# Two modulation vectors as one-column products: weights as the left operand, summed over all input tiles in PSUM

## The chip, the cores and the metric

The kernel runs on one core of a Trainium2 chip. The metric is the device time of one execution in microseconds (us). Besides DMA, five engines work side by side, each through its own queue of instructions: PE (matrix products into PSUM; PEld is its loading of the left operand), DVE and ACT (elementwise work, both read PSUM), POOL (elementwise work in SBUF) and SP, which here issues the weight transfers. They wait for one another through semaphores.

## The reference, cut to what matters

The program is a two-layer encoder over 256 positions of width 2048: an RWKV-7 layer, then a band-attention layer, each with an MLP. A vector `c` modulates every sub-layer.

```python
D_MODEL = 2048; SEQ = 256; DEPTH = 2
def modulate(h, shift, scale):
    return h * (1 + scale[:, None, :]) + shift[:, None, :]

for layer in range(DEPTH):
    mod = c @ w_ada[layer] + b_ada[layer]            # (1, 6 * 2048)
    sh1, sc1, gt1, sh2, sc2, gt2 = jnp.split(mod, 6, axis=-1)
    ...
    h = modulate(rms_norm(x, g_mix[layer]), sh1, sc1)
    y = rwkv7_time_mix(h, ...)      # layer 0: v = (h + xx * mu[3]) @ w_v, and so on
    x = x + gt1[:, None, :] * y
    h = modulate(rms_norm(x, g_mlp[layer]), sh2, sc2)
    x = x + gt2[:, None, :] * sq_relu_mlp(h, w_up[layer], w_down[layer])
return rms_norm(x, g_final)
```

The change concerns `sh1` and `sc1` of layer 0 alone: 2 x 2048 numbers, each a sum over 2048 inputs, from 32 MB of f32 weights.

## The kernel before, in words

Everything is laid out with features on the 128 partitions: a vector of 2048 is a [128, 16] tile whose column n is "tile n", and activations are [128, 16, 256]. Large products are made of fp32r halves: a weight tile is split by `halves` into wH (ACT, L362) and wL (DVE, L365), an activation by `split` into two halves (ACT L536, DVE L537), and three partial products are summed in PSUM.

The first stage is `layer_a` (L593), about the first 220 us. It computes `sh1` and `sc1` (parts 0 and 1) in eight blocks of two tiles, in the generator `ada_blocks` (L623). For each block and part, four transfers of 512 KB (L635, tile `rawa`, four buffers) bring [128 inputs, 4 input tiles, 256 outputs] each, so a block has eight transfers and the stage 64. For each of the four input tiles one f32 product (L639) has 32 copies of `c`'s column (tile `crep`, made once by DVE at L617) as its left operand and 256 columns of weights as the moving one. Input tile kt uses column tile kt mod 4 of the array (`tile_position=(0, g)`), so four products stand side by side, and the sums lie in PSUM as rows: 32 equal rows for each of four groups of input tiles. After 16 input tiles ACT copies the rows to SBUF (L645), and 16 products of one column with the constant 1/32 (L650, `col(C_32ND)`) turn them into columns and add up the four groups. DVE adds the bias (L656, twice) and makes the gain (L658).

The PSUM tile of these sums, tag `m`, has one buffer; the norm's `rstd` (L489) uses it too. The norm of the first tile needs the first block, and tile n of the norm needs block n/2: DVE scales (L718), ACT shifts (L720), POOL makes the difference to the position before (L675), DVE mixes (L680), then PE runs the LoRA products (L727, L731, f32) and the value products: `v` (L735 to L737, by rows, 24 a tile) and `t` (`v_part`, L699 to L701, 24 a tile from tile 4 on), whose sums ACT copies (L705) or DVE adds (L707).

The order on each engine is made by a scheduler from the order of issue; the generator is advanced in the loop over tiles (L709), one transfer's products at a time, ahead of the tile that needs the block. Later modulation vectors are made in another way: DVE accumulates the weighted rows (L425), and `ada_sum` (L432) turns them into columns with 32 one-column products (L437), whose left operand is 32 columns of the accumulated tile. The rest (RWKV pairs, output product, MLP, attention) is not touched by the diff.

## Time and profile before

| what | value |
|---|---|
| median of 3 runs | 2769.86 us (2765.64 to 2773.61) |
| the profiled execution | 2776.48 us, of which the span from first to last instruction is 2774.7 |
| PE busy | 2666.3 us, 96% |
| DVE, ACT, POOL busy | 2120.3 us (76%), 1277.1 (46%), 286.7 (10%) |
| HBM traffic | 237 GB/s over the span |
| mean granted TensorE clock | 0.986 |

The views: the page sums an execution up. "Groups" put the instructions of one line and shape together: count, busy time, mean ns of one, then the idle time of the engine before them and what ended it (`<-`). "Windows" give each engine's busy time, with the number of its records, in a stretch of time. "In order of time" lists one engine's instructions with start and length, like ones merged (`x8`). A product's left operand of "128x32" has 128 rows and 32 columns; an f32 product leaves more than one MATMUL record. "issue" as a releaser means that the engine waited for nothing that the profile shows.

### The profile page before, as it was taken

To read this page: it belongs to the slowest core of one execution; us is meant where nothing else is said; L and a number is where in the kernel's file an instruction comes from. 1 tells how busy PE (TensorE), PEld (TensorE's weight loads), DVE (VectorE), ACT (ScalarE), POOL (GpSimd) and SP (SyncE) were. 2 spreads that over 40 slices of the span, in tenths; PEclk is the share of its full clock that TensorE was granted. 3 is DMA by queue.
4 is the path that set the end of the run, shared out by engine and by line. 5 is a ranking of instruction groups with operands and counts; after the bars stand their busy time and mean duration, and the time that the engine had idled before them with its cause. 6 is when DMAs were issued, how large, how long until landed. Compare 5 with 4: busy or idle time off the path is not lost.

```text
span 2774.7 us, 58075 instructions
## 1 busy us (share of the span) xinstructions
PE 2666.3 (96%) x23594; PEld 2236.9 (81%) x23594; DVE 2120.3 (76%) x3161; ACT 1277.1 (46%) x2253; POOL 286.7 (10%) x416
## 2 busy tenths in 40 slices
PE   6999999999999999999999999998999999999997
PEld 3677777777888888888888888776888888888886
DVE  4568678788899888788888997799997566565665
ACT  2345455555445434344344454465454344443454
POOL 0003343353210000000000100000100000000002
PEclk9999999999999999999999999999999999999999
DMA  9876456554686889898898878888867555555553
GB/s 300 279 268 193 153 184 190 169 182 150 211 303 226 304 304 304 292 308 306 299 313 288 294 245 278 277 264 271 282 229 269 184 189 188 185 189 185 187 188 123
DMA packets 217389, 662.62 MB, mean 239 GB/s; under 512 B 21409, under 2 KB 68897, under 8 KB 217121
## 3 DMA queue, kind: packets, MB, share of 16 engines
q1 hardware_dynamic: 215056, 656.36, 71.3%
q8 instruction: 185, 3.03, 0.4%
q10 hardware_dynamic: 2064, 2.54, 0.3%
q14 instruction: 84, 0.68, 0.1%
HBM read 656.72 MB, written 2.10 MB: 237 GB/s over the span
## 4 chain that ended last, share of the span: by engine, by line
PE 79%; DVE 7%; DMA 6%; issue 4%; ACT 2%; POOL 1%; DVEq 0%; ACTq 0%; POOLq 0%
PE pj L396 41%; PE pj L397 21%; DMA raw<-w_ada 3%; DVE wL L365 3%; DMA raw<-w_ada_kv 2%; PE iv L105 2%; PE gr L99 1%; DVE acc L425 1%; PE m L639 1%; PE o L385 1%; PE ms L99 1%; ACT wH L362 1%; POOL sL L117 1%; PE o L387 1%; PE py L320 1%
## 5 line engine op out<-in xcount | busy, mean ns | idle before, releaser
L396 PE MATMUL pj<-aHL,wH 128*128 128x512 f32 x3520 | 1282.1, 404 | 8.7 <-ACT wH L362 6.5
L362 ACT CAST wH<-raw 128x1024 fp32r<-128x1024 f32 x772 | 807.2, 1046 | 973.2 <-PE pj L396 611.2
L365 DVE TENSOR_TENSOR wL<-raw,wH 128x1024 fp32r<-128x1024 f32 x772 | 943.6, 1225 | 270.7 <-ACT wH L362 267.8
L397 PE MATMUL pj<-aHL,wL 128*128 128x256 f32 x3520 | 993.2, 282 | 2.4 <-DVE wL L365 2.3
L396 PEld LDWEIGHTS pj<-aHL,wH 128*128 128x128 f32 x3520 | 666.5, 189 | 170.3 <-issue 10.1
L396 PE MATMUL pj<-hHL,wH 128*128 128x512 f32 x2048 | 725.4, 399 | 4.3 <-DVE hHL L906 4.3
L397 PEld LDWEIGHTS pj<-aHL,wL 128*128 128x128 f32 x3520 | 666.7, 189 | 5.6 <-DVE wL L365 4.0
L397 PE MATMUL pj<-hHL,wL 128*128 128x256 f32 x2048 | 574.6, 281 | 4.8 <-DVE wL L365 4.7
L425 DVE SCALAR_TENSOR_TENSOR acc<-raw,ct,acc 128x1024 f32<-128x1024 f32 x360 | 467.0, 1297 | 123.5 <-DMA raw<-w_ada 83.3
L396 PEld LDWEIGHTS pj<-hHL,wH 128*128 128x128 f32 x2048 | 385.3, 188 | 100.4 <-DVE hHL L906 6.7
L397 PEld LDWEIGHTS pj<-hHL,wL 128*128 128x128 f32 x2048 | 387.4, 189 | 7.1 <-DVE wL L365 6.7
L484 POOL TENSOR_TENSOR ss<-ss,sq 128x256 f32<-128x256 f32 x56 | 52.0, 929 | 1615.5 <-ACT sq L483 1615.2
L931 DVE SCALAR_TENSOR_TENSOR x<-pj,mod,x 128x256 f32<-128x256 f32 x256 | 123.2, 481 | 51.6 <-PE pj L397 48.6
L905 ACT CAST hHL<-t 128x256 fp32r<-128x256 f32 x128 | 51.6, 403 | 61.2 <-DVE t L904 60.2
L639 PE MATMUL m<-rawa,crep 128*32 128x256 f32 x512 | 47.2, 448 | 16.8 <-DMA rawa<-w_ada 16.3
L387 PE MATMUL pj<-aHL,wL 128*128 128x258 f32 x192 | 55.9, 293 | 6.9 <-DVE wL L365 6.9
L385 PE MATMUL pj<-aHL,wH 128*128 128x258 f32 x192 | 56.2, 293 | 2.2 <-ACT wH L362 1.6
L386 PE MATMUL pj<-aHL,wH 128*128 128x258 f32 x192 | 56.3, 293 | 0.0
L906 DVE TENSOR_TENSOR hHL<-t,hHL 128x256 fp32r<-128x256 f32 x128 | 53.4, 417 | 1.4 <-ACT hHL L905 1.4
L904 DVE SCALAR_TENSOR_TENSOR t<-t 128x256 f32<-128x256 f32 x120 | 50.7, 422 | 2.7
L881 DVE TENSOR_TENSOR t<-pj,t 128x256 f32<-128x256 f32 x120 | 50.0, 417 | 0.5 <-ACT t L880 0.5
L241 POOL TENSOR_TENSOR al<-da,csts 128x128 f32<-128x128 f32 x64 | 41.1, 652 | 68.8 <-PE iv L105 64.1
(246 smaller groups left out, 2792.6 us busy)
## 6 DMA issues: line engine op xcount, KB each, us to landing
raw<-w_ada SPq DMA_DIRECT2D x320, 512.0 KB, 4.9
raw<-w_up SPq DMA_DIRECT2D x256, 512.0 KB, 4.8
raw<-w_down SPq DMA_DIRECT2D x256, 512.0 KB, 4.3
rawa<-w_ada SPq DMA_DIRECT2D x64, 512.0 KB, 6.6
raw<-w_ada_kv SPq DMA_DIRECT2D x64, 512.0 KB, 5.6
raw<-w_k SPq DMA_DIRECT2D x32, 512.0 KB, 4.4
raw<-w_r SPq DMA_DIRECT2D x32, 512.0 KB, 4.6
raw<-w_o SPq DMA_DIRECT2D x32, 512.0 KB, 5.0
```

Source lines behind the costliest of these rows:

```text
L99: self.b.nc.tensor.matmul(o(c)[K], lhsT(c)[K], rhs(c)[K], start=True, stop=True)
L105: self.b.nc.tensor.matmul(o[QS[K], c, :], lhsT[QS[R], c, :], rhs[QS[R], c, :], start=True, stop=True, tile_position=(H * R, H * K))
L362: nc.scalar.copy(Hf, raw)
L365: eng.tensor_tensor(out=Lf, in0=raw, in1=Hf, op=ALU.subtract)
L385: nc.tensor.matmul(ps, H[:, i, :], a(kt)[:, 0, :], start=(first and kt == 0), stop=False)
L386: nc.tensor.matmul(ps, H[:, i, :], a(kt)[:, 1, :], start=False, stop=False)
L387: ins = nc.tensor.matmul(ps, L[:, i, :], a(kt)[:, 0, :], start=False, stop=(last and kt == KT - 1))
L396: nc.tensor.matmul(ps, H[:, i, :], a(kt), start=(kt == 0), stop=False)
L397: ins = nc.tensor.matmul(ps[:, 0, :], L[:, i, :], a(kt)[:, 0, :], start=False, stop=(kt == KT - 1))
L425: nc.vector.scalar_tensor_tensor(out=acc, in0=raw, scalar=ck, in1=acc, op0=ALU.mult, op1=ALU.add)
L639: nc.tensor.matmul(ps[g:g + 32, part, :W], crep[:, kt, :], raw[:, i, :], start=(part == 1 and kt < 4), stop=(part == 0 and kt >= KT - 4), ...
L931: nc.vector.scalar_tensor_tensor(out=x, in0=ps[:, i, :], scalar=self.mods[(layer, 5)][:, n:n + 1], in1=x, op0=ALU.mult, op1=ALU.add)
```

## The change

Weights and `c` swap places. A product now has 32 columns of the weights as its left operand and one column of `c` as the moving one, so that its sum is already a column of 32 outputs. The four column tiles of the array are the four groups of 32 outputs of a tile. All 16 input tiles add up in the same PSUM column; column `part * w_ + n` of the tile `m` holds part `part` of the block's n-th tile. A transfer has 4 input tiles x 2 tiles x 4 groups = 32 such products in place of 4, so 2048 in place of 256 over the stage. `crep`, the copy `adat`, the 128 products with 1/32 and that constant are gone, and the bias is added from the first PSUM tile.

```diff
-    put("cols", np.tile(np.array([RMS_EPS, GN_EPS, -0.5, 1.0, 1 / 32], np.float32), (P, 1)))
+    put("cols", np.tile(np.array([RMS_EPS, GN_EPS, -0.5, 1.0], np.float32), (P, 1)))
...
-            crep = pb.tile([P, KT, 32], F32, name="crep")
-            nc.vector.tensor_copy(crep, self.ct.unsqueeze(2).to_broadcast([P, KT, 32]))
...
-                    ps = self.psm().rearrange("p (i n) -> p i n", i=2)
+                    ps = self.psm()
...
                                 kt = ks * a + i
-                                g = 32 * (kt % 4)
-                                nc.tensor.matmul(ps[g:g + 32, part, :W], crep[:, kt, :], raw[:, i, :],
-                                                 start=(part == 1 and kt < 4), stop=(part == 0 and kt >= KT - 4),
-                                                 tile_position=(0, g))
+                                for n in range(w_):
+                                    for g in range(0, P, 32):
+                                        nc.tensor.matmul(ps[g:g + 32, part * w_ + n:part * w_ + n + 1],
+                                                         raw[:, i, n * P + g:n * P + g + 32], self.ct[:, kt:kt + 1],
+                                                         start=(part == 1 and kt == 0 and n == 0),
+                                                         stop=(part == 0 and kt == KT - 1 and n == w_ - 1),
+                                                         tile_position=(0, g))
...
-                    t = pb.tile([P, 2 * T], F32, tag="adat", bufs=1, name="adat").rearrange("p (i n) -> p i n", i=2)
-                    nc.scalar.copy(t[:, :, :W], ps[:, :, :W])
-                    ps = self.psm()
-                    for part in range(2):
-                        for i in range(w_):
-                            for g in range(0, P, 32):
-                                nc.tensor.matmul(ps[g:g + 32, 2 * part + i:2 * part + i + 1],
-                                                 t[:, part, i * P + g:i * P + g + 32], self.col(C_32ND),
-                                                 start=True, stop=True, tile_position=(0, g))
...
-                        nc.vector.tensor_tensor(out=self.mods[(0, part)][:, o], in0=ps[:, 2 * part:2 * part + w_],
+                        nc.vector.tensor_tensor(out=self.mods[(0, part)][:, o], in0=ps[:, part * w_:(part + 1) * w_],
```

In the changed file the new products are at L638, the adds of the bias at L648.

More of the change, by code (lines that the diff above doesn't have):

```diff
@@ L72 @@
 QS = [slice(H * i, H * i + H) for i in range(4)]
-C_RMS, C_GN, C_MHALF, C_ONE, C_32ND = range(5)
+C_RMS, C_GN, C_MHALF, C_ONE = range(4)
 class Pair:
```

## The prediction

> **What bounds the kernel now.** I read the page first (busy shares, the DMA queues), then the groups of the first 220 us, where all the changed lines run, then that stage by windows and PE's instructions in order of time.

> ```profile
> span 2774.7 us, 58075 instructions
> ...
> PE 2666.3 (96%) x23594; PEld 2236.9 (81%) x23594; DVE 2120.3 (76%) x3161; ACT 1277.1 (46%) x2253; POOL 286.7 (10%) x416
> ...
> q8 instruction: 185, 3.03, 0.4%
> ```
> ```profile
> L639 PE MATMUL m<-rawa,crep 128*32 128x256 f32 x512 | 47.2, 448 | 16.8 <-DMA rawa<-w_ada 16.3 <-DVE rv L491 0.5
> L650 PE MATMUL m<-csts,adat 128*32 128x1 f32 x256 | 3.6, 175 | 0.9 <-ACT adat L645 0.9
> ```
> ```profile
> core 0: us, PE busy (x) PEld busy (x) DVE busy (x) ACT busy (x) POOL busy (x), PEclk, DMA share, GB/s
> 97.00:118.00 21.00, 20.13 (x188) 14.65 (x191) 10.54 (x20) 6.28 (x11) 1.34 (x2) 1.00 0.82 286
> 142.00:165.00 23.00, 21.41 (x206) 15.86 (x207) 13.97 (x30) 7.23 (x12) 1.88 (x2) 1.00 0.92 310
> ```

> PE is busy 96% of the span, and within the first stage 20.13 of 21 us and 21.41 of 23. So there too PE sets the pace: what a changed product costs in PE's order is paid, and DVE and ACT, half idle, matter only where PE waits for them. The first 25 us are paced by DMA instead (below). The groups show 512 records for 256 products of L639 and 256 records for 128 of L650: an f32 product makes two MATMUL records, and as many LDWEIGHTS.

> **The change part by part.** Per 512 KB transfer of weights, four products that move 256 columns (L639) become 32 that move one (L638 of the changed file), with tile shape and operands like L437, which this kernel already runs in batches of 32. Per block of two tiles, one ACT copy (L645) and 16 products (L650) go. There are 64 transfers and eight blocks; SP's and POOL's queues keep their order, so no DMA moves past another.

> *PE time of a batch*, from PE's instructions in order of time: the old batch, the new batch's likeness, and the removed one.

> ```profile
> 151.34 0.28 PE L737 MATMUL v<-aHL,wL 128*128 128x256 f32 x1
> 151.55 0.64 PE L639 MATMUL m<-rawa,crep 128*32 128x256 f32 x8
> 152.12 0.39 PE L735 MATMUL v<-aHL,wH 128*128 128x256 f32 x1
> 152.34 0.28 PE L736 MATMUL v<-aHL,wH 128*128 128x256 f32 x1
> 152.46 0.28 PE L737 MATMUL v<-aHL,wL 128*128 128x256 f32 x1
> ```
> ```profile
> 913.14 0.28 PE L397 MATMUL pj<-aHL,wL 128*128 128x256 f32 x1
> 913.34 0.71 PE L437 MATMUL m<-csts,acc 128*32 128x1 f32 x64
> 913.99 0.50 PE L396 MATMUL pj<-aHL,wH 128*128 128x512 f32 x1
> 914.32 0.28 PE L397 MATMUL pj<-aHL,wL 128*128 128x256 f32 x1
> 914.44 0.40 PE L396 MATMUL pj<-aHL,wH 128*128 128x512 f32 x1
> 914.68 0.28 PE L397 MATMUL pj<-aHL,wL 128*128 128x256 f32 x1
> ```
> ```profile
> 164.00 0.28 PE L699 MATMUL t<-aHL,wH 128*128 128x256 f32 x1
> 164.22 0.43 PE L650 MATMUL m<-csts,adat 128*32 128x1 f32 x32
> 164.80 0.28 PE L701 MATMUL t<-aHL,wL 128*128 128x256 f32 x1
> ```

> Undisturbed starts are 0.12 us apart (152.34, 152.46). With four L639 products between, 151.34 to 152.34 is 1.00 where two starts make 0.24: the batch costs 0.76 us. With 32 L437 products, 913.14 to 914.32 is 1.18 where a wide and a narrow pitch (914.32 to 914.68) make 0.36: 0.82, so +0.06 a transfer. The L650 batch costs 0.80 - 0.24 = 0.56. In seven blocks that run against a dense PE: 56 x 0.06 - 7 x 0.56 = 3.4 - 3.9 = **-0.5 us**. On PE time the change is a tie.

> Accumulating one column over 16 tiles has no row here (L437 starts and stops each product). Its bounds: 0 (L437's two records already add into one address), and at most the old 0.76 doubled, since four column tiles overlap either way. I take 0.

> [...] 64 MATMUL records took 0.65 us, 10 ns each. [...]

> *The shorter chain at a block's end.* The modulation waits for the block's last product.

> ```profile
> 92.90 0.64 PE L639 MATMUL m<-rawa,crep 128*32 128x256 f32 x8
> 94.38 0.43 PE L650 MATMUL m<-csts,adat 128*32 128x1 f32 x32
> 97.23 0.39 PE L699 MATMUL t<-aHL,wH 128*128 128x256 f32 x1 [0.79 <-ACT v L705]
> 99.08 0.67 PE L727 MATMUL l<-mix,lw 128*96 128x256 f32 x2 [0.63 <-DVE mix L680]
> ```

> From the end of L650 (94.81) to the first L727 of the next tile are 4.3 us, through DVE, ACT and POOL; PE waits 0.79 + 0.63 = 1.42 of them. The change starts this 4.3 at the last product instead, 1.3 us earlier (93.47 to 94.81). But in the new order the 26 products of v that stood on both sides of L650 all follow the last product: 3.1 us of cover against 4.3, a wait of 1.2 instead of 1.42. That is -0.2 x 7 = **-1.5 us**. Bounds: 0, and the full 1.3 x 7 = -9.

> *The start.*

> ```profile
> 20.88 1.08 PE L639 MATMUL m<-rawa,crep 128*32 128x256 f32 x8 [0.42 <-DMA rawa<-w_ada]
> 22.38 1.08 PE L639 MATMUL m<-rawa,crep 128*32 128x256 f32 x8 [0.42 <-DMA rawa<-w_ada]
> 25.00 0.58 ACT L645 COPY adat<-m 128x512 f32<-128x512 f32 x1 [6.54 <-PE m L639]
> 25.64 0.60 PE L650 MATMUL m<-csts,adat 128*32 128x1 f32 x32 [0.70 <-ACT adat L645]
> ```

> The first block's transfers come 1.5 us apart and nothing covers its end: copy and L650 (25.00 to 26.24) go, -1.2. The copy of crep (L617) is off the path, since L639 waited for its weights.

> *What the change adds that no busy time shows: PE's instructions themselves.* The page has 23594 + 23594 PE and PEld records, and queue q8 brought 185 packets, 3.03 MB: 255 records, 16 KB a packet. So q8 is PE's instruction stream, in blocks of 256. It can be late:

> ```profile
> 264.39 0.34 PE L105 MATMUL iv<-u,xs 32*32 32x32 f32 x17
> 264.99 0.38 PE L105 MATMUL iv<-u,xs 32*32 32x32 f32 x15 [0.27 <-issue]
> ```
> ```profile
> 738.12 0.38 PE L105 MATMUL iv<-u,xs 32*32 32x32 f32 x20
> 738.88 0.31 PE L105 MATMUL iv<-u,xs 32*32 32x32 f32 x12 [0.38 <-issue]
> ```
> ```profile
> 264.98:362.98 98.00, 93.32 (x1651) 71.50 (x1651) 70.68 (x129) 45.83 (x126) 40.01 (x49) 0.91 0.53 166
> 362.98:738.87 375.89, 369.80 (x7115) 288.89 (x7115) 304.52 (x566) 198.32 (x557) 149.31 (x200) 0.99 0.57 178
> 262.76:266.14 3.38, 2.65 (x70) 2.10 (x71) 3.38 (x8) 0.98 (x3) 2.25 (x2) 0.85 0.54 162
> 733.05:736.43 3.38, 3.38 (x101) 2.79 (x90) 2.35 (x4) 1.69 (x4) 0.00 (x0) 1.00 0.88 316
> ```

> Batches of 32 independent products break off in the middle, with "issue" as the only releaser, at 264.99, 363.00 and 738.88. Between the breaks lie 3302 and 14230 records, 26 and 106 short of 13 and 56 blocks of 256; PE's semaphore instructions fill that up. So each break stands at a block's border. The DMA view, narrowed to 0.01 or 0.02 us, finds one q8 packet at 262.76 (its row:

> ```profile
> q8 instruction: 1, 0.02, 603.8%
> ```

> Before, the stage fetched 12 blocks in 186 us, which hid every round:

> ```profile
> q8 instruction: 12, 0.20, 0.5%
> ```

> The new products make 4 records each: (2048 - 256 - 128) x 4 = 6656 more, 26 more blocks. Inside a run of new batches, one batch and the 8.5 products of v after it are 128 + 17 records in 0.82 + 8.5 x 0.12 = 1.8 us, so 256 in 3.2 us: less than a round. A block's eight batches stand in two runs (five and three) and hold (8 x 128 + 6 x 17)/256 = 4.4 instruction blocks; the first of each run was fetched during the stretch before it, leaving 2.4. The stage's DMA share, 0.82 to 0.92, is like the slow round, but a stopped PE releases no buffers and thins the DMA, so I take the middle round, 4.6: 2.4 x (4.6 - 3.2) x 7 = **+24 us**. At 3.4 it is 2.4 x 0.2 x 7 = +3, at 5.7 +42. At the start eight batches are four blocks, at two transfers (3.0 us) each; two of them must be fetched: 2 x 1.6 = +3.2, with the -1.2 above **+2**.

> [...]

> Sum: -0.5 - 1.5 + 24 + 2 = +24 on the profiled execution's 2776.5 us. That stands 6.6 above the median; on the median of 2769.9 it gives 2794.

> **The rivals.** *Fetches stay hidden* (more than one block ahead, the three breaks chance): -0.5 - 1.5 - 1.2 = -3, **2767**. For it: no break in the stage before. Against: two breaks exactly whole blocks from the first. Chance 0.16.
> *Faster:* fetches hidden, and each block's end gains its whole 1.3 us, because PE waits for the chain and nothing else: -9 - 1.2 - 0.5 = -11, **2759**. It decides from 1 us a block's end on. Against: the new order puts the same 26 products there, and one of the two waits was for ACT's L705, not the chain. Chance 0.05.
> *The granted clock falls*, since a one-column batch keeps the array emptier. For it: a cold L639 batch (1.08 us at 20.88, 0.64 at 151.55) shows that PE does slow after sparse work. Against: the L437 and L650 batches left the next pitch at 0.12. If a quarter of the seven blocks' 96 products x 0.12 = 11.5 us doubled: +20 without any late fetch, **2790**. Chance 0.08.
> [...]

> **How the numbers follow.** Late fetches get 0.69, of which 0.03 lie at rounds near 3.4 us, below +8. A change under 0.3% (8.3 us) can't be told from none. Slower: 0.66 + 0.08 + 0.02 = 0.76; same 0.16 + 0.03 = 0.19; faster 0.05. The range runs from the hidden fetch (2767) past the slow round (-0.5 - 1.5 + 42 with a start of +4: 2814) to 2820. For late fetches alone it would be 2772 to 2814.

> **What would show it.** Right: q8 with 211 packets, PE with 26922 records; batches of L638 broken off inside by "issue" without any releaser; PEld's idle time by "issue" up by tens of us; blocks of 25 to 27 us instead of 23 (94.38 to 164.22, three blocks); all later stages as long as before. Wrong: L638 batches unbroken at 0.65 us each and blocks of 23 us (hidden); pitches of 0.24 in v's products between batches (clock); batches evenly stretched to 1.6 us (floor).

## The result and the profile after

The changed kernel takes 2816.84 us (median; 2814.87 to 2820.34) against 2769.56 us before: a ratio of 1.017, 95% interval 1.0152 to 1.0187, so 47 us slower. The profiled execution took 2820.34 us.

From the page of the changed kernel, the lines that answer to the first fence of the prediction:

```profile
span 2818.6 us, 64722 instructions
...
PE 2691.7 (96%) x26922; PEld 2289.7 (81%) x26922; DVE 2120.5 (75%) x3160; ACT 1272.3 (45%) x2245; POOL 293.7 (10%) x416
...
q8 instruction: 211, 3.46, 0.5%
```

PE's records rise by 3328, PEld's by as many, and q8 brings 26 packets more: the forecast's 26922 and 211 exactly. PE's share stands at 96% in both kernels. A share of busy time does not show this loss.

Windows show where it lies. First the kernel before, its first stage from 26 us on and everything behind it; then the changed kernel (columns as in the prediction; the last three are granted clock, DMA share and GB/s):

```profile
26.00:220.00 194.00, 177.20 (x1591) 131.24 (x1584) 112.46 (x219) 68.62 (x107) 14.41 (x16) 0.98 0.81 271
220.00:2774.00 2554.00, 2480.10 (x21928) 2103.65 (x21926) 2000.94 (x2926) 1199.90 (x2129) 272.07 (x396) 0.99 0.71 236
```
```profile
30.00:261.00 231.00, 201.37 (x4487) 178.50 (x4482) 112.70 (x218) 64.94 (x99) 13.73 (x16) 0.85 0.69 225
261.00:2818.00 2557.00, 2481.93 (x21928) 2103.41 (x21928) 2001.39 (x2927) 1199.67 (x2130) 279.73 (x396) 0.99 0.71 235
```

Behind the first stage both run the same 21928 PE records in 2554 and 2557 us. The first stage, without its start, went from 194 to 231 us, its start from 26 to 30: 41 of the profiled span's 44 us. Two things are new in that row: PE is idle for 30 us instead of 17, and the granted clock (that column of the windows, a share of full speed) is 0.85 instead of 0.98. The pace of the blocks stands in the starts of the bias adds (first and last start of 16 instructions, two a block), before and after:

```profile
L656 DVE TENSOR_TENSOR mod<-m,bada x16: 147/154/160, 26.3 to 187.6; 128x2 f32<-128x2 f32 x16
```
```profile
L648 DVE TENSOR_TENSOR mod<-m,bada x16: 147/156/160, 30.1 to 229.4; 128x2 f32<-128x2 f32 x16
```

Seven blocks in 161.3 us are 23.0 each; in 199.3 us, 28.5 each.

The groups of the new products on the changed kernel's page, and PE's instructions in order of time at three places:

```profile
L638 PE MATMUL m<-ct,rawa 128*32 128x1 f32 x4096 | 55.0, 180 | 37.1 <-issue 19.2
L638 PEld LDWEIGHTS m<-ct,rawa 128*32 128x32 f32 x4096 | 48.8, 127 | 48.8 <-issue 34.7
```
```profile
23.22 1.49 PE L638 MATMUL m<-ct,rawa 128*32 128x1 f32 x97 [0.56 <-issue]
...
29.41 0.64 PE L638 MATMUL m<-ct,rawa 128*32 128x1 f32 x33 [3.78 <-issue]
...
53.69 0.71 PE L638 MATMUL m<-ct,rawa 128*32 128x1 f32 x64
54.33 0.39 PE L728 MATMUL v<-aHL,wH 128*128 128x256 f32 x1
...
122.98 0.63 PE L638 MATMUL m<-ct,rawa 128*32 128x1 f32 x56 [1.00 <-issue]
...
124.02 0.41 PE L728 MATMUL v<-aHL,wH 128*128 128x256 f32 x1
124.24 0.42 PE L729 MATMUL v<-aHL,wL 128*128 128x256 f32 x1
...
125.44 1.03 PE L638 MATMUL m<-ct,rawa 128*32 128x1 f32 x63
129.45 0.16 PE L638 MATMUL m<-ct,rawa 128*32 128x1 f32 x1 [2.98 <-issue]
```

An undisturbed batch takes 0.64 us (53.69 to 54.33), as the batch of L437 did. But batches are broken off inside by "issue", and always at the same place in PE's instruction stream: with PE's and PEld's records and PE's semaphore instructions counted together from the start, each of the 14 breaks of over 0.1 us in the whole run stands at record 193 of a block of 256. The three breaks of the kernel before, on which the prediction built, stand at record 193 too. Twelve of the 14 lie in the first stage, which crosses 39 such borders; two of these twelve (69.52 and 143.14) fall between wide products of v and t and not inside a batch. From one break to the next PE got 256 instructions in 6.2 us (23.22 to 29.41) and in 6.5 us (122.98 to 129.45). And between the breaks PE is at times cold, that is, at a lower granted clock (0.58 from 122.98 to 129.45): two products of v start 0.22 us apart instead of 0.12, and 63 records take 1.03 us instead of 0.64.

### The profile page after: what moved, and what is told of

Same layout as the page of the kernel before. It is cut to its first block, busy times and chain, and to the rows that moved or that the text cites. A ratio compares the mean times of both kernels' runs of the same rounds, so it can differ in the third digit from the quotient of the medians.

```text
span 2818.6 us, 64722 instructions
## 1 busy us (share of the span) xinstructions
PE 2691.7 (96%) x26922; PEld 2289.7 (81%) x26922; DVE 2120.5 (75%) x3160; ACT 1272.3 (45%) x2245; POOL 293.7 (10%) x416
## 4 chain that ended last, share of the span: by engine, by line
PE 74%; DMA 10%; DVE 9%; issue 5%; ACT 1%; POOL 1%; DVEq 0%; SPq 0%; ACTq 0%; POOLq 0%
PE pj L396 36%; PE pj L397 18%; DMA raw<-w_ada 5%; DMA raw<-w_ada_kv 4%; DVE wL L365 3%; PE iv L105 2%; DVE acc L425 2%; PE m L638 1%; PE gr L99 1%; PE o L385 1%; PE ms L99 1%; PE l L719 1%; PE v L728 1%; POOL sL L117 1%; PE v L729 1%
## 5 line engine op out<-in xcount | busy, mean ns | idle before, releaser
L396 PE MATMUL pj<-aHL,wH 128*128 128x512 f32 x3520 | 1284.8, 405 | 6.4 <-ACT wH L362 4.0
L397 PE MATMUL pj<-aHL,wL 128*128 128x256 f32 x3520 | 994.8, 283 | 5.2 <-DVE wL L365 5.0
L396 PEld LDWEIGHTS pj<-aHL,wH 128*128 128x128 f32 x3520 | 667.7, 190 | 168.1 <-issue 10.4
L396 PE MATMUL pj<-hHL,wH 128*128 128x512 f32 x2048 | 723.1, 398 | 2.6 <-DVE hHL L898 2.6
L397 PEld LDWEIGHTS pj<-aHL,wL 128*128 128x128 f32 x3520 | 668.0, 190 | 10.5 <-DVE wL L365 8.9
L397 PE MATMUL pj<-hHL,wL 128*128 128x256 f32 x2048 | 574.1, 281 | 4.8 <-DVE wL L365 4.6
L396 PEld LDWEIGHTS pj<-hHL,wH 128*128 128x128 f32 x2048 | 384.5, 188 | 97.1 <-DVE hHL L898 5.0
L397 PEld LDWEIGHTS pj<-hHL,wL 128*128 128x128 f32 x2048 | 386.5, 189 | 8.6 <-DVE wL L365 8.3
L638 PE MATMUL m<-ct,rawa 128*32 128x1 f32 x4096 | 55.0, 180 | 37.1 <-issue 19.2
L638 PEld LDWEIGHTS m<-ct,rawa 128*32 128x32 f32 x4096 | 48.8, 127 | 48.8 <-issue 34.7
```

What stands on the lines that cost most here:

```text
L396: nc.tensor.matmul(ps, H[:, i, :], a(kt), start=(kt == 0), stop=False)
L397: ins = nc.tensor.matmul(ps[:, 0, :], L[:, i, :], a(kt)[:, 0, :], start=False, stop=(kt == KT - 1))
L638: nc.tensor.matmul(ps[g:g + 32, part * w_ + n:part * w_ + n + 1], raw[:, i, n * P + g:n * P + g + 32], self.ct[:, kt:kt + 1], start=(part ...
```

## The experiments

Every time below is a median of its runs, beside runs of the kernel before on the same chip, whose medians were 2770.2 to 2771.3; ratios with their 95% intervals. Two theories stood first: *late fetches* (PE uses its instructions faster than q8 brings them) and *clock* (one-column products lower the granted clock).

### 1. Wider left operands, fewer instructions

```diff
-                                    for g in range(0, P, 32):
-                                        nc.tensor.matmul(ps[g:g + 32, part * w_ + n:part * w_ + n + 1],
-                                                         raw[:, i, n * P + g:n * P + g + 32], self.ct[:, kt:kt + 1],
+                                    for g in range(0, P, 64):
+                                        nc.tensor.matmul(ps[g:g + 64, part * w_ + n:part * w_ + n + 1],
+                                                         raw[:, i, n * P + g:n * P + g + 64], self.ct[:, kt:kt + 1],
```

That is 64 columns, 16 products a transfer; with 128 columns there are 8 and no column tiles.

> Edit: the changed kernel with 64 columns of weights as the left operand, 16 products and 64 PE records a transfer, same sums. Late fetches: 736 records a block (2.9 instruction blocks of 256), at rounds of 5.9 us 17 us, under the 23 us of PE work: breaks by 'issue' nearly gone, q8 about 195 packets, 2772 to 2795 us. One-column products as such: the clock stays low and the time near the changed kernel's 2817.

> Edit: the changed kernel with 128 columns of weights as the left operand, so 8 products a transfer in place of 32, same sums, 32 PE records a transfer in place of 128. Late instruction fetches: a block of the stage holds 480 records (1.9 blocks of 256 in 23 us), so no batch breaks off with 'issue' as releaser, q8 has about 187 packets, and what is left is PE time: two MATMUL records a product at the 0.06 to 0.12 us pitch of single products, 1.1 to 2.1 us a batch in place of 0.76: 2790 to 2845 us in all, with the granted clock back at 0.98 in the stage. One-column products as such (an empty array lowers the clock, or a floor for each product): the clock stays at 0.73 to 0.90 from 50 to 250 us as in the changed kernel.

Measured: 64 columns 2855.04 us, 1.0302 (1.0280 to 1.0324); 128 columns 2914.84 us, 1.0539 (1.0485 to 1.0594). Both times lie above all that were expected: with fewer instructions the kernel became slower still. In order of time, a batch of 64 columns and of 128 columns, each followed by the next product of v:

```profile
153.76 1.10 PE L638 MATMUL m<-ct,rawa 128*64 128x1 f32 x32
154.79 0.39 PE L727 MATMUL v<-aHL,wH 128*128 128x256 f32 x1
```
```profile
151.82 1.84 PE L637 MATMUL m<-ct,rawa 128*128 128x1 f32 x16
153.53 0.36 PE L725 MATMUL v<-aHL,wH 128*128 128x256 f32 x1
```

From start to next start the batch takes 1.03 and 1.71 us instead of 0.64: here four narrow products side by side were cheaper than one wide one. Over 56 batches that is some +22 and +60. The windows show the rest:

```profile
104.80:118.40 13.60, 13.60 (x102) 12.24 (x102) 2.36 (x2) 2.48 (x3) 0.00 (x0) 0.50 0.83 290
100.00:150.00 50.00, 49.93 (x541) 44.95 (x541) 15.52 (x33) 8.96 (x15) 1.40 (x2) 0.68 0.69 230
```

These are the 64 columns: PE is busy for 49.93 of 50 us at a clock of 0.68, and in one stretch for 13.60 of 13.60 us at 0.50. No batch breaks off at a block's border here, so the fetches are on time, and still the clock is down. So the clock fell here without late fetches; my expectation, that it would come back, was wrong. Since the price of the batch changed too, the run does not say what late fetches cost.

### 2. A quarter of the bytes

```diff
-                            raw = pb.tile([P, HK * P], F32, tag="rawa", bufs=4, name="rawa")
+                            raw = pb.tile([P, HK * P // 4], F32, tag="rawa", bufs=4, name="rawa")
...
-                            nc.sync.dma_start(out=raw, in_=w[a])
+                            nc.sync.dma_start(out=raw, in_=w[a][:, :, 0:W // 4])
...
-                                                         raw[:, i, n * P + g:n * P + g + 32], self.ct[:, kt:kt + 1],
+                                                         raw[:, i, g % 64:g % 64 + 32], self.ct[:, kt:kt + 1],
```

> Edit: the changed kernel, same products on PE, but each transfer brings only the first quarter of its columns (128 KB in place of 512 KB) and the products use these columns over again; so the modulation is not the reference's. Late fetches made long by a busy DMA: a round falls from 5.9 us toward 3.4, PE's time by block from 29 toward 23 to 24 us: 2765 to 2785. Rounds that do not depend on DMA load, or one-column products as such: blocks stay at 28 to 29 us, 2805 to 2817.

Measured: 2813.26 us, 1.0144 (1.0114 to 1.0174). The time hardly moved, and so lies where the other theories had it. The rounds (from one block's arrival to the next, with PE waiting) did move; PE's instructions in order of time, and the windows that hold them:

```profile
16.61 1.88 PE L638 MATMUL m<-ct,rawa 128*32 128x1 f32 x128 [2.63 <-issue]
20.61 1.88 PE L638 MATMUL m<-ct,rawa 128*32 128x1 f32 x128 [2.12 <-issue]
24.62 0.55 PE L638 MATMUL m<-ct,rawa 128*32 128x1 f32 x28 [2.12 <-issue]
...
34.18 1.89 PE L638 MATMUL m<-ct,rawa 128*32 128x1 f32 x128 [1.61 <-issue]
37.63 1.88 PE L638 MATMUL m<-ct,rawa 128*32 128x1 f32 x128 [1.57 <-issue]
41.09 1.08 PE L638 MATMUL m<-ct,rawa 128*32 128x1 f32 x68 [1.57 <-issue]
```
```profile
16.50:24.60 8.10, 3.77 (x256) 3.60 (x256) 0.00 (x0) 0.00 (x0) 0.00 (x0) 1.00 0.51 126
34.00:41.20 7.20, 3.88 (x264) 3.72 (x268) 5.16 (x11) 1.31 (x3) 1.18 (x2) 1.00 0.33 69
```

This is the plainest picture of the stops: 128 MATMUL records (with their 128 loads one block of 256), a stop, 128, a stop. The round is 4.0 us at a DMA share of 0.51 and 3.45 us at 0.33, against 6.2 to 6.5 in the changed kernel. (The clock column reads 1.00 in the first 40 us of the traces whatever the pace: 128 records take 1.88 us in these rows, and 1.33 in experiment 4.) That the time stayed has another reason than the expectation had in mind: the order of PE's products changed with the smaller transfers. In the changed kernel every batch but the first eleven stands alone between wide products; here all but six of the 48 behind the first sixteen stand in groups of three or four, and the stops at borders in the first stage sum to 41 us instead of 24. So the run shows shorter rounds on a quieter DMA, and settles nothing about the total.

### 3. Half the products

Part 1 is made as before, part 0 as changed.

```diff
+                                if part:
+                                    g = 32 * (kt % 4)
+                                    nc.tensor.matmul(rows[g:g + 32, :W], crep[:, kt, :], raw[:, i, :],
+                                                     start=(kt < 4), stop=(kt >= KT - 4), tile_position=(0, g))
+                                else:
+                                    for n in range(w_):
...
+                            if part and a == KT // ks - 1:
+                                t = pb.tile([P, T], F32, tag="adat", bufs=1, name="adat")
+                                nc.scalar.copy(t[:, :W], rows[:, :W])
+                                ps = self.psm()
```

> Edit: the kernel before for part 1 (rows, copy, products with 1/32) and the changed one for part 0, which ends a block. Four of a block's eight transfers carry 128 records each: 864 records a block (3.4 instruction blocks), at rounds of 5.9 us 20 us against 23 us of PE work, in a run of two to four batches. Late fetches: one break of 1 to 3 us a block at most, start 0 to +2, chain at a block's end -0.2 to -1.3 us: 2762 to 2790. One-column products as such: half of the change's loss, about 2793.

Measured: 2794.36 us, 1.0083 (1.0057 to 1.0109): 23 us, half the loss for half the products. That is the figure expected of one-column products as such, and just above the 2790 of late fetches, so the time alone does not speak for the fetches. The borders still stop PE:

```profile
70.48 0.29 PE L645 MATMUL m<-ct,rawa 128*32 128x1 f32 x10
73.31 0.92 PE L645 MATMUL m<-ct,rawa 128*32 128x1 f32 x54 [2.54 <-issue]
```

One batch of 64 records breaks after its tenth. With half the new instructions the average demand is well below a round's supply (26 packets of q8 between 20 and 239 us, one in 8.4 us), and still a run of batches is enough for a stop. In all I count seven such stops in the first stage, 15 us.

### 4. The clock kept up

The moved operand becomes 32 equal columns of `c`; the number of products stays.

```diff
+            crep = pb.tile([P, KT, 32], F32, name="crep")
+            nc.vector.tensor_copy(crep, self.ct.unsqueeze(2).to_broadcast([P, KT, 32]))
...
-                                        nc.tensor.matmul(ps[g:g + 32, part * w_ + n:part * w_ + n + 1],
-                                                         raw[:, i, n * P + g:n * P + g + 32], self.ct[:, kt:kt + 1],
+                                        nc.tensor.matmul(ps[g:g + 32, part * w_ + n, :],
+                                                         raw[:, i, n * P + g:n * P + g + 32], crep[:, kt, :],
...
```

> Edit: the changed kernel, but each product moves 32 equal columns of c (the tile crep) in place of one, and column 0 of the 32 sums is used: same products, same PE records, same DMA, same sums. If emptiness of the moving side lowers the clock (one column in flight), 32 columns lift the granted clock in the stage from 0.73 to 0.90 toward 1.0 and the cold pitches go: 12 to 20 us less than the changed kernel, 2797 to 2805, while the breaks at instruction blocks stay (about 26 us). If the stops at instruction blocks alone make PE cold, or late fetches are all, clock and time stay: 2812 to 2822.

Measured: 2808.06 us, 1.0136 (1.0117 to 1.0156), some 9 us less than the changed kernel (2 to 17 by the two intervals), between the two expected ranges. From 100 us on the granted clock is 0.94 to 1.00, where the changed kernel had 0.83 to 0.90. PE, in order of time:

```profile
114.26 1.11 PE L640 MATMUL m<-crep,rawa 128*32 128x32 f32 x103
115.60 1.33 PE L640 MATMUL m<-crep,rawa 128*32 128x32 f32 x128 [0.23 <-issue]
120.70 0.47 PE L640 MATMUL m<-crep,rawa 128*32 128x32 f32 x25 [3.76 <-issue]
```

128 records take 1.33 us, warm, and then PE stands 3.76 us for its next block. The stops at borders in the first stage grew from 24 us to 41. But the order of the products did not stay: these three rows follow one another, 256 records or four batches without a wide product between, and 35 of the 53 batches behind the first eleven stand in groups of two to four, where the changed kernel has each alone. Experiment 2, with one column moved and the batches grouped much alike, also has 41 us of stops. So the longer stops can come from the order alone, and the 9 us are no measure of what the clock costs. What the run does show is the clock: beside experiment 2, whose transfers differ and which had 0.83, 0.85 and 0.91 in the three windows of 50 us from 100 us on, the 32 columns had 0.94, 0.95 and 1.00.

### 5. Bursts against a trickle, in another place

The kernel before, with 96 extra one-column products in each of 48 tiles of the second MLP, in one batch or in four of 24. `columns` makes four products for each column that it is given. Same products, same records.

```diff
-                self.proj2(ps, w, lambda kt: hl[:, kt, :, 0:T])
+                self.proj2(ps, w, lambda kt: hl[:, kt, :, 0:T], (0, 8))
+                if extra:
+                    columns(dummy, 0, 24)
+                self.proj2(ps, w, lambda kt: hl[:, kt, :, 0:T], (8, KT))
```
```diff
-                self.proj2(ps, w, lambda kt: hl[:, kt, :, 0:T])
+                for k4 in range(0, KT, 4):
+                    self.proj2(ps, w, lambda kt: hl[:, kt, :, 0:T], (k4, k4 + 4))
+                    if extra:
+                        columns(dummy, 3 * k4 // 2, 3 * k4 // 2 + 6)
```

> Edit: the kernel before with 96 added one-column products (left operand 32 columns of constants) in the middle of each of the 48 hidden tiles of the second MLP's last three quarters, in one batch; their sums are not used. DMA is quiet there (share 0.59). PE price 96 x 0.0175 + 0.2 = 1.9 us a batch, 90 us in all. Late fetches: 384 records of a batch hold one or two borders of 256; where two, the second comes 1.1 us after the first and PE stops for a round of 3.4 to 3.8 us less that, about 2.5 us in half of the batches: 90 + 48 x 0.5 x 2.5 = +150 us, and more than e6_spread. [...]

> Edit: as e6_burst, with the same 96 products a tile in four batches of 24, one after every four input tiles: same products, records and DMA. Three more drains of 0.2 us a tile: 96 x 0.0175 + 4 x 0.2 = 2.5 us, +120 us in all. Late fetches: 448 records in 8 us of a tile are 4.6 us a block, more than a round of 3.8: no breaks by issue, +120 us, which is some 30 us less than e6_burst. No late fetches: +120 us, 30 us more than e6_burst. One-column products as such lower the clock: both kernels show a granted clock under 0.95 from 2300 us on, and cost more than these sums.

Measured: one batch 2949.58 us, 1.0645 (1.0625 to 1.0664); four batches 2903.99 us, 1.0484 (1.0462 to 1.0505). The burst is 46 us dearer, with 257 packets on q8 in both. (Both cost more than expected, 179 us against 150 and 134 against 120; the difference has the expected sign.) The burst's PE in order of time, then a window of the burst and of the trickle:

```profile
2254.24 1.63 PE L894 MATMUL m<-csts 128*32 128x1 f32 x174
2259.34 0.43 PE L894 MATMUL m<-csts 128*32 128x1 f32 x18 [3.47 <-issue]
...
2260.50 0.63 PE L396 MATMUL pj<-aHL,wH 128*128 128x512 f32 x1
```
```profile
2300.00:2350.00 50.00, 45.24 (x1141) 39.14 (x1140) 17.89 (x26) 14.60 (x22) 0.00 (x0) 0.91 0.31 108
```
```profile
2300.00:2350.00 50.00, 50.00 (x1343) 40.58 (x1342) 21.56 (x30) 16.18 (x23) 0.00 (x0) 1.00 0.37 129
```

The burst stops 3.47 us inside a batch, and the next wide product is cold (0.63 us instead of the 0.40 in the prediction's rows). The trickle never stops and keeps the clock at 1.00. By my count the burst's stops at borders sum to some 50 us, about the difference. Here, where the DMA share is only 0.31 to 0.37 in these windows and where nothing of the changed stage runs, the same instructions cost a stop or none, by their spacing alone.

### 6. The old chain, taken away

The kernel before without ACT's copy and the products with 1/32.

```diff
-                    nc.scalar.copy(t[:, :, :W], ps[:, :, :W])
...
-                                nc.tensor.matmul(ps[g:g + 32, 2 * part + i:2 * part + i + 1],
-                                                 t[:, part, i * P + g:i * P + g + 32], self.col(C_32ND),
...
```

> Edit: the kernel before without ACT's copy of the sums and without the products with 1/32; the bias is added to two columns of the sums in rows, so the modulation is not the reference's. It takes what the change can give (PE time of 128 products, the shorter chain at a block's end and at the start) without what it adds. By the prediction's steps: 7 x 0.56 = 3.9 us of PE, 1.5 (bounds 0 and 9) of chain, 1.2 at the start: 6.6 us less than before, 2763; by the faster rival's full chain 14 us less, 2755.

Measured: 2768.13 us, 0.9989 (0.9976 to 1.0002), so -3 us (-7 to +1) by the ratio. That is what the removed steps could give back: PE's time for L650, the shorter chain, and the copy at the start. The forecast's -3.9 - 1.5 - 1.2 = -6.6 lies at the edge of the interval; whether the gain is that or nothing this experiment cannot tell, but a large one it excludes.

### 7. Half the instructions, the rest kept

The upper half of each f32 weight is read in place as bf16, and `c` is rounded to bf16. Transfers, column tiles and the single moved column stay, and but for a product here and there the order.

```diff
+            ctb = pb.tile([P, KT], BF16, name="ctb")
+            nc.vector.tensor_copy(ctb, self.ct)
...
+                            top = raw.bitcast(BF16).rearrange("p i (n t) -> p i n t", t=2)[:, :, :, 1]
...
-                                                         raw[:, i, n * P + g:n * P + g + 32], self.ct[:, kt:kt + 1],
+                                                         top[:, i, n * P + g:n * P + g + 32], ctb[:, kt:kt + 1],
```

> The changed kernel with the same 2048 products in the same order, but on the upper halves of the f32 weights, read as bf16, and on c rounded to bf16: a product then makes one MATMUL and one LDWEIGHTS record instead of two and two, so 64 instructions a transfer instead of 128. Transfers, bytes, column tiles and the single moved column are as in the changed kernel; sh1 and sc1 are only as exact as bf16. Late fetches: q8 195 packets; a block of two tiles holds some 1330 - 512 records, 3.2 instruction blocks, at 5.9 us each 19 us, less than its 23 us of PE time, so PE is not bound by its instructions on average, and in a run of five batches 256 records last 4.4 to 5.7 us against a round of 6 to 6.7, so at most some 1 us of stops a block. Time 2750 to 2780, that is, the loss of 47 us all but gone. Granted clock: as many one-column products as before keep the array as empty, so the clock stays at 0.73 to 0.90 in this stage and v's products cold; at least the 10 to 15 us of cold pitches stay: 2780 to 2800. A price of the small products as such, whatever their number of instructions: 2800 or more.

Measured: 2754.16 us, 0.9950 (0.9933 to 0.9968): not only is the loss gone, the kernel is 17 us faster by the medians (9 to 19 by the interval) than the one before, at sums only as exact as bf16. From its page, its windows, what the new products waited for (us, times; the changed kernel's line of the same view stands second), and one batch in order of time:

```profile
q8 instruction: 195, 3.19, 0.5%
```
```profile
26.00:216.00 190.00, 171.01 (x2764) 147.06 (x2765) 123.80 (x241) 76.07 (x125) 14.69 (x19) 0.98 0.86 290
```
```profile
  issue: 6.5, 16
```
```profile
  issue: 54.0, 42
```
```profile
118.83 0.28 PE L696 MATMUL t<-aHL,wH 128*128 128x256 f32 x1
119.04 0.36 PE L642 MATMUL m<-ctb,rawa 128*32 128x1 bf16 x32
119.33 0.39 PE L697 MATMUL t<-aHL,wL 128*128 128x256 f32 x1
119.56 0.28 PE L695 MATMUL t<-aHL,wH 128*128 128x256 f32 x1
119.67 0.28 PE L696 MATMUL t<-aHL,wH 128*128 128x256 f32 x1
```

"issue" falls from 54.0 us to 6.5 (PE's and PEld's waits added up, so that a stop can count twice), the clock is back at 0.98, the DMA share up from 0.69 to 0.86. The time also closes as a sum. From 118.83 to 119.67 are 0.84 us; three pitches make 0.36, so a batch costs 0.48 where the old L639 batch cost 0.76: 56 x -0.28 = -16, and with experiment 6's -3 for the removed steps -19; measured -9 to -19. No price for the form of the products is left over that these runs could show.

The clock is the one thing this run does not part from the instructions: a shorter batch also fills less of PE's time with one-column work. No run here parts the two with the order of the products kept.

## Why the prediction was right, and which term it left out

The direction, the mechanism and the place held; 2817 lies in the range (2767 to 2820), at its upper end, and 23 above the 2794. That it lies inside is partly luck: the upper end was worked out for a slower round (2814) and for a rival (2820), and what filled it was in good part the clock.

**PE time of a batch: right.** An unbroken batch takes 0.64 us, where L437's 64 records took 0.65. Accumulating over 16 tiles costs nothing that a row shows. The 2820 that ends the range, 0.02 of the chances and the last line's batches of 1.6 us stand for a floor under the pitch of the products, which no run shows: 64 records take 0.64 us, 10 ns each, and warm batches are not stretched.

**Removed steps and start: small, as said.** Experiment 6 gives -3 for what the forecast put at -6.6. The faster rival needed -3.9 - 9 - 1.2 = -14 from the same steps, and that is outside its interval. The start, forecast +2, came to +3.8 (bias add at 30.1 instead of 26.3).

**Late fetches: the right term, near its size, but not by its factors.** The forecast had 2.4 blocks x (4.6 - 3.2) x 7 = +24, that is, 17 stops of 1.4 us. In the seven blocks PE stopped at 10 borders, 20 us in all, 2.0 us each. The middle round of 4.6, with the reason that "a stopped PE releases no buffers and thins the DMA", was too short: five times a stop follows a stop at the very next border, 6.05 to 6.75 us later, and in four of the five rounds the DMA share was 0.94 to 1.07, as in this window (columns as above):

```profile
122.98:129.45 6.47, 3.49 (x128) 3.17 (x128) 1.22 (x1) 1.05 (x1) 0.00 (x0) 0.58 1.07 370
```

Fewer borders than forecast stopped PE, and so two errors nearly cancel. A count suggests why most borders did not: q8 brought 37 packets between 20 and 250 us,

```profile
q8 instruction: 37, 0.61, 1.1%
```

one in 6.2 us, about the round itself. On average the instructions just came in time; only runs of batches used them faster.

That the fetches stay hidden, a rival at 0.16, is contradicted for dense small products by the 14 stops of the changed kernel, and by those of experiments 2 to 4 (41, 15 and 41 us in the first stage) and of the burst (some 50 us); for the trickle, which never stopped, it holds.

**The clock: left out of the sum, because it was taken for an alternative.** It had 0.08 as the cause in place of late fetches. It came on top: pitches of 0.22 in v's products, 0.73 granted between 50 and 100 us,

```profile
50.00:100.00 50.00, 43.20 (x1141) 36.20 (x1144) 21.71 (x47) 10.06 (x17) 3.09 (x4) 0.73 0.69 223
```

and products that take longer. Windows can be asked for the products of one tile alone: stretch, PE's busy time with them, clock, DMA share, GB/s. Here for v, before and after, up to the first product of the next stage:

```profile
0.00:219.68 219.68, 61.20 (x384) 0.98 0.83 277
0.00:261.13 261.13, 71.40 (x384) 0.87 0.72 235
```

With t (54.4 and 60.3) and the LoRA products (37.2 and 41.1), the same 896 records take 172.8 us instead of 152.9. So the stage's 41 us are, on PE, 23.5 of waiting for instructions, 20 of slower wide products and 4 more in the products of `m` (52.0 and 56.2), less 6 of other waits. The forecast had 24 for the fetches or 20 for the clock; the case was about both, side by side.

They do not look independent. Between 60 and 220 us the changed kernel has six stretches at half the clock, of 7 to 20 us. Five begin in a stop at a border or within 1 us behind it; this one, with 1.00 granted from 134.3 to 154.6, began in a stop of 2.44 us:

```profile
155.11 0.72 PE L638 MATMUL m<-ct,rawa 128*32 128x1 f32 x41 [2.44 <-issue]
```
```profile
154.70:164.90 10.20, 9.79 (x136) 8.92 (x136) 2.01 (x3) 2.09 (x2) 0.00 (x0) 0.50 0.92 314
```

But experiment 1 lost the clock without such stops. How much of the 20 us would stay if the instructions came in time, no run here shows; that stays open.

Both signs that the prediction named were there at once: batches broken by "issue" (PEld's idle time by it is 34.7 us, of which 9.4 lie ahead of its first instruction), and cold pitches.

## What to carry to other kernels

Count PE's instructions, not only its time: an f32 product left four records in these traces (two MATMUL, two LDWEIGHTS), and where 256 of them lasted less than a round of the instruction queue (3.45 to 6.75 us), PE stood still, up to 3.81 us at a border in the changed kernel, however cheap each product was. Before many tiny products replace a few wide ones, work out instructions per microsecond for each run of them; if they must come, let them trickle between wide products (no stop in experiment 5), or take a type that makes fewer records (in experiment 7 bf16 left 2048 MATMUL records where f32 left 4096). After an edit, look at PE's order as well: in experiments 2 and 4 it changed along with the thing that was to be tested. "issue" as the only releaser, in the middle of a batch of independent products and a whole number of blocks from the next such break, is the sign to look for.

## What the runs showed of the hardware that was not expected

The round was longer on a busier DMA, and by more than I allowed: 3.45 us at a share of 0.33 and 4.0 at 0.51 (experiment 2), 6.2 and 6.5 at 1.03 and 1.07 (changed kernel). The share alone does not set it: in experiment 4 one round took 4.55 us at 0.91 and another 6.10 at 0.62.

A stage of one-column products lost its clock even where PE never rested: 0.68 with PE busy 49.93 of 50 us (experiment 1). With 32 equal columns moved instead of one, at the same 10 ns a record, the clock was 0.94 and more (experiment 4) where it was 0.83 to 0.91 with one (experiment 2), in a similar order of products but with other transfers. Batches of 24 products between wide ones left it at 1.00 (experiment 5), and bf16 products, one column each, at 0.98 (experiment 7).

Four 32-column products side by side were cheaper here than the same work in one product of 128 columns: 0.64 against 1.71 us a transfer for the same weights (changed kernel and experiment 1).
